# The w_down product of a transformer block by seven block products instead of eight

## The chip, the core and the metric

The kernel runs on one core of a Trainium2 chip. The metric is the time of one launch in device microseconds (us). The engines that matter here are TensorE (PE in the profile, its weight loads PEld), VectorE (DVE), ScalarE (ACT) and the queues that issue DMAs (SP above all). Each engine works through its own list of instructions in order; semaphores hold an instruction until what it needs is there.

## The reference

One layer of a hybrid block, in float32, on 512 tokens of 2048 features. Ahead of the part that is changed stand three mixers (retention, mLSTM, S5), an output projection and a layer norm. The changed part is the feed-forward, and what reads it:

```python
x = layer_norm(ALPHA * x + mix, ln1_w, ln1_b)
ff = jnp.matmul(jnp.square(jax.nn.relu(jnp.matmul(x, w_up))), w_down)
r = ALPHA * x + ff
ple = jax.nn.sigmoid(jnp.matmul(r, w_gate)) * jnp.matmul(p_l, w_ple)
return layer_norm(r + ple, ln2_w, ln2_b)
```

`w_up` is 2048 x 8192, `w_down` 8192 x 2048, `w_gate` 2048 x 2048.

## The kernel before

Activations stand feature-major: a tile is 128 features (partitions) by 512 tokens. Every float32 operand of a large product is split into a high part (a copy by ACT, rounded to the type that TensorE reads, `acp` in `split`, L123) and a low part (a subtraction by DVE, L127), and every product is made of three matmuls, high x high, high x low and low x high (`mm3`, L141 to L143). In them the weight is the stationary operand and 512 tokens of activations move, so a matmul's result is 128 output features by 512 tokens in one PSUM bank.

Weights come as blocks of 128 x 1024 float32 (512 KB), laid out on the host in the order of their use. `wblk` loads one by a DMA on SP's queue (four buffers), and splits it into `wh` and `wl` (three buffers each). One block feeds 24 matmuls. `gemm` runs over blocks.

The feed-forward goes in 16 rounds, `c`. `up(c)` makes four hidden tiles of 128 features in four PSUM banks (tags `mm` and `bu`) from 8 blocks of `w_up`, each of which holds 2 input tiles by 4 hidden tiles; ReLU is ACT's, the square (`tt(r, r, r, MUL)`) and the low part DVE's. `down(c, hs)` takes 8 blocks of `w_down`, two output tiles each, into the banks `wk` and `ya`, and adds each of the 16 banks to its tile `acc[k]` in SBUF by DVE (L114). `acc[k]` held the normed input, so `down(0)` also scales it by ALPHA. `up(c + 1)` is written ahead of `down(c)`, so that TensorE has 192 matmuls (round 0) or 384 (later rounds) of other products between a hidden tile's last matmul and its first use.

After the last round each `acc[k]` is split (`rh`, `rl`) and added to `sd`, the sum over features; the gate product (`gate`, 8 groups) reads all 16 split tiles.

Instructions are put in each engine's list by a list scheduler at build time, from the dependences, the order of writing and the priorities given by `tc.high_priority`; on the chip that list is fixed.

## Time and profile before

| | us |
|---|---|
| median of 3 runs | 2493.32 |
| lowest and highest run | 2492.93, 2493.97 |
| span of the profiled execution, first to last instruction | 2491.1 |
| first matmul on the normed input (feed-forward begins) | 885.2 |
| first matmul of the gate product | 2279.8 |

The profiled execution's time is known by its span; it lies 2.2 us under the median of the runs. The profile's busy time of an engine is the time in which at least one of its instructions is in work. Matmuls overlap, so a busy TensorE need not be at its peak: the distance between the starts of two matmuls says more than their durations. The same holds in a small way for DVE, whose next instruction starts somewhat before the end of the one in work.

### The profile page before, as it was taken

How to read it: one execution, taken by the hardware profiler on the slowest of the kernel's cores; microseconds unless marked ns; L12 is line 12 of the kernel's file. 1: busy time of each engine (PE TensorE's matmuls, PEld its weight loads, DVE VectorE, ACT ScalarE, POOL GpSimd, SP SyncE). 2: the span in 40 equal slices, each digit the busy share in tenths (PEclk: the TensorE clock that was granted, in tenths of full speed). 3: DMA queues.
4: the chain of work that ended last, by engine and by line, in shares of the span. 5: the costliest groups of instructions: out<-in, count | busy, mean ns of one | idle time of the engine just before them, and what ended most of it. 6: DMA issues, size and time to landing. Idle time of an engine off the chain costs nothing.

```text
span 2491.1 us, 29260 instructions
## 1 busy us (share of the span) xinstructions
PE 2454.7 (99%) x11443; PEld 2051.7 (82%) x11443; DVE 1407.6 (57%) x2357; ACT 823.0 (33%) x1187; POOL 89.5 (4%) x182
## 2 busy tenths in 40 slices
PE   9999999999999999999999999999999999999996
PEld 7888888888888878888888888888888888888896
DVE  6788889897654564344334334433433443358477
ACT  4544444444432362122222212222221222123354
POOL 4100000000000000000000000000000000000002
PEclk9999999999999999999999999999999999999998
DMA  6433343333533443333333333332333333233364
GB/s 229 147 107 100 108 121 100 112 100 105 179 119 124 138 127 102 93 101 93 98 98 96 99 94 101 93 101 94 101 94 97 98 94 101 93 102 93 119 188 143
DMA packets 94618, 280.47 MB, mean 113 GB/s; under 512 B 11232, under 2 KB 19856, under 8 KB 94480
## 3 DMA queue, kind: packets, MB, share of 16 engines
q1 hardware_dynamic: 80752, 257.10, 33.1%
q10 hardware_dynamic: 8352, 13.11, 1.6%
q0 software_dynamic: 5376, 8.39, 1.3%
q8 instruction: 90, 1.47, 0.3%
q14 instruction: 48, 0.39, 0.1%
HBM read 264.12 MB, written 14.44 MB: 112 GB/s over the span
## 4 chain that ended last, share of the span: by engine, by line
PE 95%; DVE 2%; DMA 1%; issue 1%; ACT 0%; POOL 0%; ACTq 0%; SPq 0%; DVEq 0%
PE mm L141 14%; PE mm L143 14%; PE mm L142 14%; PE bu L141 7%; PE bu L143 7%; PE bu L142 7%; PE wk L141 7%; PE wk L142 7%; PE wk L143 7%; PE ya L141 2%; PE ya L142 2%; PE ya L143 2%; DMA pldr<-t 1%; PE ya L546 1%; PE wk L620 0%
## 5 line engine op out<-in xcount | busy, mean ns | idle before, releaser
L127 DVE TENSOR_TENSOR wl<-raw,wh 128x1024 fp32r<-128x1024 f32 (+1 forms) x449 | 548.6, 1222 | 641.0 <-ACT wh L123 634.7
L123 ACT ACTIVATE wh<-raw 128x1024 fp32r<-128x1024 f32 (+1 forms) x449 | 474.5, 1057 | 1301.7 <-PE bu L142 573.4
L141 PE MATMUL mm<-xh,wh 128*128 128x512 f32 x800 | 317.3, 397 | 5.5 <-ACT wh L123 5.5
L143 PE MATMUL mm<-xh,wl 128*128 128x512 f32 x800 | 312.9, 391 | 0.0
L142 PE MATMUL mm<-xl,wh 128*128 128x512 f32 x800 | 312.1, 390 | 0.0
L141 PE MATMUL wk<-hh,wh 128*128 128x512 f32 x768 | 298.8, 389 | 0.0
L142 PE MATMUL wk<-hl,wh 128*128 128x512 f32 x768 | 298.8, 389 | 0.0
L143 PE MATMUL wk<-hh,wl 128*128 128x512 f32 x768 | 298.8, 389 | 0.0
L114 DVE TENSOR_TENSOR acc<-acc,wk 128x512 f32<-128x512 f32 (+1 forms) x218 | 142.0, 658 | 151.0 <-PE wk L143 148.4
L141 PE MATMUL mm<-x1h,wh 128*128 128x512 f32 x512 | 200.0, 391 | 1.9 <-ACT t L123 1.9
L142 PE MATMUL mm<-x1l,wh 128*128 128x512 f32 x512 | 199.9, 390 | 0.0
L143 PE MATMUL mm<-x1h,wl 128*128 128x512 f32 x512 | 199.5, 390 | 0.0
L142 PE MATMUL bu<-x1l,wh 128*128 128x512 f32 x512 | 199.2, 389 | 0.0
L143 PE MATMUL bu<-x1h,wl 128*128 128x512 f32 x512 | 199.2, 389 | 0.0
L141 PE MATMUL bu<-x1h,wh 128*128 128x512 f32 x512 | 199.1, 389 | 0.0
L141 PEld LDWEIGHTS mm<-xh,wh 128*128 128x128 f32 x800 | 150.5, 188 | 34.9 <-ACT wh L123 5.5
L143 PEld LDWEIGHTS mm<-xh,wl 128*128 128x128 f32 x800 | 150.4, 188 | 32.0 <-DVE wl L127 0.2
L142 PEld LDWEIGHTS mm<-xl,wh 128*128 128x128 f32 x800 | 150.8, 188 | 29.9
L142 PEld LDWEIGHTS wk<-hl,wh 128*128 128x128 f32 x768 | 144.3, 188 | 29.9
L141 PEld LDWEIGHTS wk<-hh,wh 128*128 128x128 f32 x768 | 144.1, 188 | 30.0
L143 PEld LDWEIGHTS wk<-hh,wl 128*128 128x128 f32 x768 | 144.2, 188 | 29.9
L141 PEld LDWEIGHTS mm<-x1h,wh 128*128 128x128 f32 x512 | 96.5, 189 | 22.4 <-ACT t L123 2.3
(405 smaller groups left out, 3638.5 us busy)
## 6 DMA issues: line engine op xcount, KB each, us to landing
raw<-in_wall_dram SPq DMA_DIRECT2D x447, 512.0 KB, 3.5
xr<-in_xT_dram SPq DMA_DIRECT2D x16, 256.0 KB, 4.3
us<-udr POOLq DMA_DIRECT2D x64, 64.0 KB, 2.3
xr<-in_xT_dram ACTq DMA_DIRECT2D x16, 256.0 KB, 4.0
pldr<-t ACTq DMA_DIRECT2D x16, 256.0 KB, 4.1
out_dram<-acc SPq DMA_DIRECT2D x32, 128.0 KB, 1.8
r<-ydr SPq DMA_DIRECT2D x15, 256.0 KB, 3.8
ydr<-y SPq DMA_DIRECT2D x11, 256.0 KB
```

The source lines that it names most:

```text
L114: (e or V).tensor_tensor(out=out, in0=a, in1=b, op=op)
L123: return A.activation(out=out, in_=in_, func=AF.Copy, scale=scale)
L127: pools["dve"] = V.tensor_tensor(out=lo, in0=x, in1=hi, op=SUB).ins
L141: P.matmul(out=ps, lhsT=wh, rhs=xh, start=start, stop=False)
L142: P.matmul(out=ps, lhsT=wh, rhs=xl, start=False, stop=False)
L143: pools["pe"] = P.matmul(out=ps, lhsT=wl, rhs=xh, start=False, stop=stop).ins
L546: P.matmul(out=yb, lhsT=q["c"][:, j], rhs=z, start=(s % 2 == 0 and n == 0), stop=(s % 2 == 1 and n == 3))
```

## The change

`w_down` is no longer multiplied tile by tile. In each round the hidden tiles are taken as two pairs (`q`), each pair with its tokens in two halves of 256, as a 2 x 2 matrix of blocks A (tokens by hidden features); the matching rows of `w_down` and 1024 of its columns (`p`, two halves) are a 2 x 2 matrix of blocks B. The product of two such matrices is made with seven block products in Winograd's form of Strassen's scheme. It needs four sums of blocks of A (`forms`: S1 to S4, per round and pair) and four differences of blocks of B (`less`, per round and half).

- The seven forms of A, split into `fh` and `fl`, are now stationary, 128 tokens at a time; the weights move, 512 output features at a time. A result is therefore 128 tokens by 512 output features: token-major.
- Each product (`product`) splits one 128 x 1024 block of weights or of a difference of weights, and makes 12 matmuls of it. There are 14 products per round, of 4 + 4 loaded blocks (before: 8 blocks, 24 matmuls each).
- `gather` adds each product's two banks to accumulators `accs` in SBUF. Some banks are added to by a second product without being cleared, and gathered again: 28 gathers per round (before: 16).
- `up(c, g)` makes two hidden tiles at a time from blocks of 4 input tiles by 2 hidden tiles, in two banks (`mm`), and is a generator: one of its four blocks follows every second product. The square is now done by ACT.
- After the last round `result` adds the accumulator `p1` to three others in each half (12 additions), turns each output tile back to feature-major by four transposes on TensorE, adds ALPHA times the normed input and splits the sum. The normed input has been stored to DRAM (`x1dr`) and is loaded again.
- `gate` takes the residual from the split parts: two DVE instructions per tile instead of one.

```diff
-        tt(r, r, r, MUL)
+                A.activation(out=r, in_=r, func=AF.Square)
...
+        nc.sync.dma_start(out=x1dr[k], in_=z)
+    stage.close()
...
+    def up(c, g, hs):
+        b = [bank("mm"), bank("mm")]
+        for i in range(4):
+            wh, wl = wblk(W_UP + (2 * c + g) * 4 + i)
+            for q in range(4):
+                for j in range(2):
+                    k, w = 4 * i + q, slice((2 * q + j) * 128, (2 * q + j + 1) * 128)
+                    mm3(b[j], wh[:, w], wl[:, w], *x1[k], k == 0, k == KT - 1)
+            if i < 3:
+                yield
...
+    def forms(a, b):
+        fh = ffp.tile([128, 7 * T2], F32R, tag="fh", bufs=2, name="fh")
+        fl = ffp.tile([128, 7 * T2], F32R, tag="fl", bufs=2, name="fl")
+        s = ffp.tile([128, 4 * T2], F32, tag="fs", bufs=1, name="fs")
+        p = [s[:, i * T2:(i + 1) * T2] for i in range(4)]
+        tt(p[0], a[:, T2:], b[:, T2:], ADD)
+        tt(p[1], p[0], a[:, :T2], SUB)
+        tt(p[2], a[:, :T2], a[:, T2:], SUB)
+        tt(p[3], b[:, :T2], p[1], SUB)
+        split(a[:, :T2], fh[:, :T2], fl[:, :T2])
+        split(b, fh[:, T2:3 * T2], fl[:, T2:3 * T2])
+        split(s, fh[:, 3 * T2:], fl[:, 3 * T2:])
+        return fh, fl
...
+        def product(form, src, banks, first):
+            with tc.high_priority(2000):
+                wh = whp.tile([128, 1024], F32R, tag="wh", name="wh")
+                wl = wlp.tile([128, 1024], F32R, tag="wl", name="wl")
+                split(src, wh, wl)
+            for t in range(2):
+                o = slice(form * T2 + t * C, form * T2 + (t + 1) * C)
+                for q in range(2):
+                    w = slice(q * S, (q + 1) * S)
+                    (fh, fl), st = fs[q], first and q == 0
+                    for x, y in ((fh, wh), (fh, wl), (fl, wh)):
+                        P.matmul(out=banks[t], lhsT=x[:, o], rhs=y[:, w], start=st, stop=x is fl and q == 1, skip_group_check=not first)
+                        st = False
...
+        ba = [bank("bu"), bank("bu")]
+        product(A11, b11, ba, True)
+        gather("p1", ba)
+        yield
+        less(b12, b12, b11)
+        bc_ = [bank("wk"), bank("wk")]
+        product(S1, b12, bc_, True)
+        gather("c22", bc_)
+        yield
+        less(b12, b22, b12)
+        bb = [bank("ya"), bank("wk")]
+        product(S2, b12, bb, True)
+        gather("c12", bb)
+        yield
+        product(A12, b21, ba, False)
+        gather("c11", ba)
+        yield
+        less(b11, b12, b11)
+        product(S3, b11, bb, False)
+        gather("c22", bb)
+        yield
+        product(S4, b22, bc_, False)
+        gather("c12", bc_)
+        yield
+        less(b21, b21, b12)
+        product(A22, b21, bb, False)
+        gather("c21", bb)
+        yield
...
+    def result(p):
+        for n in ("c12", "c21", "c22"):
+            for t in range(2):
+                tt(accs[p, n, t], accs[p, n, t], accs[p, "p1", t], ADD)
+        for j in range(8):
+            k = 8 * p + j
+            xr = ffp.tile([128, S], F32, tag="r", bufs=4, name="x1r")
+            nc.sync.dma_start(out=xr, in_=x1dr[k])
+            tp = bank("mm")
+            for t in range(NC):
+                src = accs[p, f"c{t // 2 + 1}{j // 4 + 1}", t % 2]
+                P.transpose(tp[:, t * C:(t + 1) * C], src[:, (j % 4) * C:(j % 4 + 1) * C], ident)
+            z = ffp.tile([128, S], F32, tag="r", bufs=4, name="z")
+            stt(z, xr, ALPHA, tp, MUL, ADD)
+            xh, xl = abuf("rh"), abuf("rl")
+            split(z, xh, xl)
...
+            tt(sd, sd, z, ADD)
...
+            d, u = down(c, p, fs), up(c + 1, p, nx) if c + 1 < NF else iter(())
+            for i, _ in enumerate(d):
+                if i % 2 == 0:
+                    next(u, None)
...
-            tt(z, z, nmean[:, sl], ADD)
+            stt(z, rr[k][0][:, sl], 1.0, nmean[:, sl], MUL, ADD)
+            tt(z, z, rr[k][1][:, sl], ADD)
```

In TensorE's list the seam between two rounds reads as follows. Before, the last matmuls of `up` (`x1h`, `x1l` with a `w_up` block) are followed by `down` on hidden tiles (`hh`, `hl`) of the round before:

```order
L142 MATMUL bu_11628<-x1l_8086,wh_11840 128x512
L143 MATMUL bu_11628<-x1h_8085,wl_11841 128x512
L141 MATMUL wk_11897<-hh_11328,wh_11900 128x512
L142 MATMUL wk_11897<-hl_11329,wh_11900 128x512
L143 MATMUL wk_11897<-hh_11328,wl_11901 128x512
```

After, the last matmul of `up` is followed by the first product of the next round, cut in pieces: `fh_11808` and `fl_11809` are the forms of the first pair, `fh_11821` those of the second pair, whose hidden tiles the matmul just ahead has finished; `mm` is the next round's `w_up`.

```order
L143 MATMUL mm_11565<-x1h_8101,wl_11774 128x512
L1029 MATMUL bu_11842<-wh_11844,fh_11808 128x512
L1029 MATMUL bu_11842<-wl_11845,fh_11808 128x512
L1029 MATMUL bu_11842<-wh_11844,fl_11809 128x512
L1029 MATMUL bu_11843<-wh_11844,fh_11808 128x512
...
L141 MATMUL mm_11862<-x1h_7975,wh_11865 128x512
L1029 MATMUL bu_11842<-wh_11844,fh_11821 128x512
L1029 MATMUL bu_11842<-wl_11845,fh_11821 128x512
...
L141 MATMUL mm_11863<-x1h_7984,wh_11865 128x512
L1029 MATMUL bu_11842<-wh_11844,fl_11822 128x512
```

So the first use of a round's last hidden tiles moved from 384 matmuls behind their end to 13 behind it. In all, the seam reads: 6 matmuls of the first product, 7 of `w_up`, 4 of the product, 9 of `w_up`, 2 of the product, 8 of `w_up`, then the second product.

DVE's list at the same seam. Before, it squares and splits four hidden tiles between the splits of weight blocks:

```order
L114 TENSOR_TENSOR r_12413<-r_12413 128x512
L114 TENSOR_TENSOR r_12420<-r_12420 128x512
L127 TENSOR_TENSOR hl_12417<-r_12413,hh_12416 128x512
L114 TENSOR_TENSOR r_12427<-r_12427 128x512
L127 TENSOR_TENSOR wl_12513<-raw_12511,wh_12512 128x1024
```

After (`r_11802`, `r_11805` are the last two hidden tiles; `fs` the sums S1 to S4; `rawd` blocks of `w_down`; `wl_11898` the split for the second product):

```order
L127 TENSOR_TENSOR wl_11866<-raw_11864,wh_11865 128x1024
L127 TENSOR_TENSOR wl_11898<-rawd_11836,wh_11897 128x1024
L114 TENSOR_TENSOR fs_11823<-r_11802 128x256
L114 TENSOR_TENSOR rawd_11836<-rawd_11838,rawd_11836 128x1024
L114 TENSOR_TENSOR fs_11823<-r_11802,r_11805 128x256
L114 TENSOR_TENSOR rawd_11834<-rawd_11836,rawd_11834 128x1024
L114 TENSOR_TENSOR fs_11823<-fs_11823,r_11802 128x256
L127 TENSOR_TENSOR fl_11822<-r_11802,fh_11821 128x256
L114 TENSOR_TENSOR fs_11823<-r_11805,fs_11823 128x256
L127 TENSOR_TENSOR fl_11822<-r_11805,fh_11821 128x512
L114 TENSOR_TENSOR acc_8420<-acc_8420,bu_11842 128x512
```

Two differences of weight blocks and one weight split now stand between the end of the hidden tiles and the low part that TensorE's next pieces need.

DVE's list at the end of the last round. Before, the split and the sum of an output tile (`rl`, `sd`) stand right behind its last addition, among the other additions of the same round:

```order
L114 TENSOR_TENSOR acc_6993<-acc_6993,wk_16589 128x512
L114 TENSOR_TENSOR sd_6429<-sd_6429,acc_6993 128x512
L127 TENSOR_TENSOR rl_16814<-acc_6993,rh_16813 128x512
L114 TENSOR_TENSOR acc_7003<-acc_7003,wk_16590 128x512
L114 TENSOR_TENSOR sd_6429<-sd_6429,acc_7003 128x512
L127 TENSOR_TENSOR wl_16695<-raw_16693,wh_16694 128x1024
```

After, all 16 output tiles stand behind the last gather, one like the next (`mm` holds the transposes, `x1r` the loaded normed input):

```order
L111 SCALAR_TENSOR_TENSOR z_17307<-x1r_17300,mm_17302 128x512
L114 TENSOR_TENSOR sd_6430<-sd_6430,z_17307 128x512
L127 TENSOR_TENSOR rl_17310<-z_17307,rh_17309 128x512
L111 SCALAR_TENSOR_TENSOR z_17321<-x1r_17314,mm_17316 128x512
L114 TENSOR_TENSOR sd_6430<-sd_6430,z_17321 128x512
```

In TensorE's list 60 of the 64 transposes stand behind the last product, and the gate's first matmul behind the last transpose: the gate's two banks are those of the transposes.

## Rows read from the trace of the kernel before

**Rows 1.** The page: busy time of the engines; shares of the chain.
```profile
PE 2454.7 (99%) x11443; PEld 2051.7 (82%) x11443; DVE 1407.6 (57%) x2357; ACT 823.0 (33%) x1187; POOL 89.5 (4%) x182
...
PE 95%; DVE 2%; DMA 1%; issue 1%; ACT 0%; POOL 0%; ACTq 0%; SPq 0%; DVEq 0%
```

**Rows 2.** Groups by line: count, busy us, mean ns, idle before.
```profile
L127 DVE TENSOR_TENSOR wl<-raw,wh 128x1024 fp32r<-128x1024 f32 x447 | 547.2, 1224 | 640.1 <-ACT wh L123 634.0 <-PE ya L546 3.4
L123 ACT ACTIVATE wh<-raw 128x1024 fp32r<-128x1024 f32 x447 | 473.2, 1059 | 1300.7 <-PE bu L142 573.4 <-PE ya L142 258.6 <-PE mm L142 210.9
...
L114 DVE TENSOR_TENSOR acc<-acc,wk 128x512 f32<-128x512 f32 x196 | 133.7, 686 | 149.4 <-PE wk L143 148.4 <-PE wk L870 1.1
...
L123 ACT ACTIVATE hh<-r 128x512 fp32r<-128x512 f32 x64 | 38.7, 632 | 35.4 <-DVE r L114 34.2
```

**Rows 3.** Timeline of TensorE in `up(1)`: start us, us, instruction.
```profile
940.20 0.39 PE L141 MATMUL bu<-x1h,wh 128*128 128x512 f32 x1
...
941.56 0.39 PE L141 MATMUL mm<-x1h,wh 128*128 128x512 f32 x1
```

**Rows 4.** Tiles `x1h` and `rh` on TensorE: ns min/median/max, first and last start.
```profile
L141 PE MATMUL mm<-x1h,wh x512: 389/389/628, 885.2 to 2190.7; 128*128 128x512 f32 x171
...
L141 PE MATMUL mm<-rh,wh x192: 278/283/395, 2279.8 to 2453.6; 128*128 128x256 f32 x128, 128*128 128x512 f32 x64
```

**Rows 5.** Timeline of DVE where it has no wait between instructions.
```profile
975.82 1.23 DVE L127 TENSOR_TENSOR wl<-raw,wh 128x1024 fp32r<-128x1024 f32 x1
976.96 0.69 DVE L127 TENSOR_TENSOR hl<-r,hh 128x512 fp32r<-128x512 f32 x1
977.56 0.68 DVE L111 SCALAR_TENSOR_TENSOR acc<-acc,wk 128x512 f32<-128x512 f32 x1
...
2295.02 3.77 DVE L114 TENSOR_TENSOR acc<-acc,nmean 128x256 f32<-128x256 f32 x11
```

**Rows 6.** Stages: length, then busy us of PE, PEld, DVE, ACT, POOL; clock; DMA.
```profile
1063.00:1500.00 437.00, 437.00 (x1929) 361.97 (x1929) 179.59 (x203) 107.51 (x123) 0.00 (x0) 1.00 0.31 97
```

**Rows 7.** Timeline of DVE while the first norm's tiles become ready.
```profile
901.30 0.68 DVE L127 TENSOR_TENSOR x1l<-acc,x1h 128x512 fp32r<-128x512 f32 x1
901.91 0.74 DVE L111 SCALAR_TENSOR_TENSOR acc<-acc,vv,q 128x512 f32<-128x512 f32 x1
902.57 0.68 DVE L127 TENSOR_TENSOR x1l<-acc,x1h 128x512 fp32r<-128x512 f32 x1
...
912.43 1.46 DVE L127 TENSOR_TENSOR x1l<-acc,x1h 128x512 fp32r<-128x512 f32 x2
```

**Rows 8.** Stages around the start of the feed-forward; the clock is ahead of the DMA share.
```profile
870.00:880.00 10.00, 7.43 (x32) 5.38 (x31) 7.36 (x11) 5.45 (x11) 0.00 (x0) 1.00 0.44 154
880.00:885.00 5.00, 3.31 (x15) 2.28 (x13) 4.71 (x8) 3.51 (x6) 0.00 (x0) 1.00 0.76 239
885.00:890.00 5.00, 4.82 (x14) 3.82 (x15) 2.56 (x4) 2.92 (x6) 0.00 (x0) 0.66 0.79 247
```

**Rows 9.** Timeline of TensorE there; idle us before an instruction in brackets.
```profile
877.44 0.50 PE L141 MATMUL mm<-ph,wh 128*128 128x512 f32 x1 [1.77 <-ACT t L123]
...
885.18 0.50 PE L141 MATMUL mm<-x1h,wh 128*128 128x512 f32 x1 [1.87 <-ACT t L123]
...
886.61 0.63 PE L143 MATMUL mm<-x1h,wl 128*128 128x512 f32 x1
887.03 0.63 PE L141 MATMUL mm<-x1h,wh 128*128 128x512 f32 x1
```

**Rows 10.** Stages at the end of the last round and in the gate, as rows 6.
```profile
2262.00:2280.00 18.00, 18.00 (x81) 14.92 (x80) 16.57 (x23) 7.45 (x11) 0.00 (x0) 1.00 0.36 113
...
2300.00:2320.00 20.00, 20.00 (x90) 16.57 (x89) 8.74 (x12) 5.48 (x8) 0.00 (x0) 1.00 0.43 132
```

**Rows 11.** DMA issues: count, KB each, median us from issue to landing.
```profile
r<-ydr SPq DMA_DIRECT2D x15, 256.0 KB, 3.8
...
xr<-pldr ACTq DMA_DIRECT2D x8, 256.0 KB, 2.9
```

**Rows 12.** Line 602, the transposes of the heads: ns min/median/max.
```profile
L602 PE MATMUL wk<-ident,kT x48: 270/273/328, 83.5 to 653.2; 128*128 128x128 f32 x48
```

More of the change, by code (lines that the diff above doesn't have):

```diff
@@ L200, in hybrid_block_kernel @@
     pldr = dr.tile([KT, 128, S], F32, name="pldr")
+    x1dr = dr.tile([KT, 128, S], F32, name="x1dr")
     def rsqrt(pl, v, n):
@@ L951, in hybrid_block_kernel @@
         x1.append((xh, xl))
-    def up(c):
-        b = [bank("mm"), bank("mm"), bank("bu"), bank("bu")]
-        gemm(W_UP + c * 8, b, x1, 4, 2)
-        hs = []
-        for j in range(4):
-            r = tmp("r", bufs=3)
+        nc.sync.dma_start(out=x1dr[k], in_=z)
+    stage.close()
+    ffp = spool("ff")
+    accs = {}
+    def up(c, g, hs):
[8 more added lines that the diff above has]
+                yield
+        for j in range(2):
+            r = ffp.tile([128, S], F32, tag="r", bufs=4, name="r")
@@ new lines, in up @@
+            hs.append(r)
+        yield
+    T2 = S // 2
+    A11, A12, A22, S1, S2, S3, S4 = range(7)
+    def forms(a, b):
[11 more added lines that the diff above has]
+        return fh, fl
@@ new lines, in down, with gather @@
+    def down(c, p, fs):
+        i = W_DOWN + (2 * c + p) * 4
+        with tc.high_priority(2000):
+            raw = []
+            for j in range(4):
+                t = ffp.tile([128, 1024], F32, tag="raw", bufs=4, name="rawd")
+                nc.sync.dma_start(out=t, in_=wall[i + j])
+                raw.append(t)
+        b11, b12, b22, b21 = raw
+        def product(form, src, banks, first):
+            with tc.high_priority(2000):
+                wh = whp.tile([128, 1024], F32R, tag="wh", name="wh")
[9 more added lines that the diff above has]
+                        st = False
+        def gather(name, banks):
+            for t in range(2):
@@ L980, in down @@
                 with tc.high_priority(400):
-                    if c == 0:
-                        stt(z, z, ALPHA, b[j], MUL, ADD)
-                    else:
-                        tt(z, z, b[j], ADD)
+                    if (p, name, t) not in accs:
+                        z = accs[p, name, t] = ffp.tile([128, S], F32, tag="acc", bufs=20, name="acc")
+                        V.tensor_copy(out=z, in_=banks[t])
+                    else:
+                        z = accs[p, name, t]
+                        tt(z, z, banks[t], ADD)
@@ new lines, in less @@
+        def less(dst, x, y):
+            with tc.high_priority(2000):
+                tt(dst, x, y, SUB)
+        ba = [bank("bu"), bank("bu")]
[11 more added lines that the diff above has]
+        gather("c12", bb)
@@ new lines, in down @@
+        yield
[12 more added lines that the diff above has]
+        gather("c21", bb)
+        yield
+    rr = []
+    def result(p):
+        for n in ("c12", "c21", "c22"):
+            for t in range(2):
+                tt(accs[p, n, t], accs[p, n, t], accs[p, "p1", t], ADD)
[11 more added lines that the diff above has]
+            split(z, xh, xl)
+            rr.append((xh, xl))
+            if k == 0:
+                V.tensor_copy(out=sd, in_=z)
+            else:
+                tt(sd, sd, z, ADD)
@@ L986, in hybrid_block_kernel @@
     NF = FT // 4
-    hs = up(0)
+    hs = []
+    for g in range(2):
+        for _ in up(0, g, hs):
+            pass
     for c in range(NF):
-        nx = up(c + 1) if c + 1 < NF else None
-        down(c, hs)
-        hs = nx
-    rr = []
-    for k in range(KT):
-        xh, xl = abuf("rh"), abuf("rl")
-        split(acc[k], xh, xl)
-        rr.append((xh, xl))
-        if k == 0:
-            V.tensor_copy(out=sd, in_=acc[k])
-        else:
-            tt(sd, sd, acc[k], ADD)
+        fs = [forms(hs[2 * q], hs[2 * q + 1]) for q in range(2)]
+        nx = []
+        for p in range(2):
+            d, u = down(c, p, fs), up(c + 1, p, nx) if c + 1 < NF else iter(())
+            for i, _ in enumerate(d):
+                if i % 2 == 0:
+                    next(u, None)
+        hs = nx
@@ L1003, in hybrid_block_kernel @@
+    result(0)
+    result(1)
+    stage.close()
+    accp = spool("acc2", KT)
+    rp_ = spool("tmp2", 2)
+    acc = [accp.tile([128, S], F32, tag="acc", name="acc") for _ in range(KT)]
+    sq = accp.tile([128, S], F32, tag="sq", bufs=1, name="sq")
     mx = col_mean(sd, "mu")
@@ L1047, in hybrid_block_kernel @@
             nc.sync.dma_start(out=out[k][:, sl], in_=z)
+    stage.close()
 def prep(i):
@@ L1069, in prep @@
     blocks += [_pack(i["s5_glu_w"][0], 2, 4), _pack(w_out, 2, 4), _pack(i["w_ple"][0], 4, 2),
-               _pack(i["w_up"][0], 4, 2)]
-    wd = i["w_down"][0]
-    blocks += [_pack(wd[c * 512:(c + 1) * 512], 2, 4) for c in range(FT // 4)]
+               _pack(i["w_up"][0], 2, 4)]
+    wd = i["w_down"][0].reshape(FT // 4, 2, 2, 128, 2, 2, 512).transpose(0, 4, 2, 5, 3, 1, 6)
+    wd = wd.reshape(FT // 4, 2, 4, 128, 1024)[:, :, [0, 1, 3, 2]]
+    blocks.append(wd.reshape(-1, 128, 1024))
     blocks.append(_pack(i["w_gate"][0], 2, 4))
```

27 lines of the change are left out of this document (8 added, 19 removed).

## The prediction

> **What bounds the kernel now.** The page comes first: TensorE is busy for 99% of the span and holds 95% of the chain that ended last, DVE is busy for 57% and ACT for 33% [rows 1]. A busy TensorE need not be at its peak, so the next view is its timeline: six matmuls after the one at 940.20 the next starts at 941.56, which is 1.36/6 = 0.2267 us from one to the next [rows 3]. The feed-forward has 16 rounds of 384 matmuls, 6144 in all; 6144 x 0.2267 = 1392.8 us. From its first matmul at 885.2 to the gate's first at 2279.8 are 1394.6 us [rows 4]. So there is 2 us of waiting in 1395: the feed-forward is bound by the number of its matmuls, and only fewer matmuls can shorten it. DVE is busy for 179.6 of 437 us there, ACT for 107.5 [rows 6]: 41% and 25%, room for more work. The price of DVE work is its spacing, not its duration: a split of 1024 columns starts at 975.82 and the next instruction at 976.96, 1.14 us; one of 512 takes 0.60; eleven of 256 take 3.77, 0.34 each [rows 5]. The durations are 1.22 and 0.69 [rows 2, 5], some 10% more.
>
> **Matmuls.** Before, w_down took 16 x 8 x 24 = 3072. After, it takes 16 rounds x 2 halves x 7 products x 12 = 2688, of the same shape (128 x 128 stationary, 512 moving, three for one). I give them the same 0.2267 us: **-384 x 0.2267 = -87.1 us**, if TensorE stays the bound. A round then is 360 matmuls, 81.6 us instead of 87.0.
>
> **DVE and ACT per round.** DVE now has 22 weight splits (8 w_up blocks, 14 products) x 1.14 = 25.1, 8 differences `less` of the same size x 1.14 = 9.1, 28 gathers x 0.60 = 16.8, and for two pairs 4 sums x 0.34 and splits of 256, 512 and 1024 columns, 2 x (1.37 + 2.08) = 6.9: together 58 us of 81.6 (64 at full durations). Before it had about 0.41 x 87 = 36. ACT has 22 copies x 1.06 [rows 2], 8 ReLUs and squares at the 0.63 of the copy of 512 [rows 2], and about 4 us of forms: some 33 of 81.6. Both fit on the mean, so away from the seams I cost this at nothing; what hides it is TensorE's 81.6 us. The buffers allow it: three `wh`/`wl`, so a split may start when the third block before it has left TensorE, and has two products (2 x 2.72 us) or a product and a w_up block (8.16 us) to be done.
>
> **The seam between rounds.** This is where cover is thin: 13 matmuls (2.95 us) instead of 384 after the last hidden tile. Let 0 be the end of the last w_up matmul. ACT: first ReLU done at 0.1, the copy for the second product (1.06) to 1.3, second ReLU 1.7, squares 2.8, first form of the second pair 3.1. TensorE has run 13 matmuls by 2.95 and waits 0.2; then 4 + 9 more to 6.1. DVE, in its listed order: the split for the second product from 1.3 to 2.45, then three sums (0.34 each), two differences (1.14 each) and the first form's low part (0.34), up to 6.15; TensorE waits 0.1. The low part of S1 is ready at 9.5; the second product asks for it at 9.6. I take **0.4 us per seam, 15 x 0.4 = +6**. Bounds: 0, and 2.2, because from the end of the last product of a round (-5.2) to the split for the next w_up block (10.6) DVE has 14.8 us of work in 15.8 us; at full durations it is late by 1.8 more. So 0 to +33.
>
> **The first w_up product.** It asks for two hidden tiles at a time, so it passes the 16 normed input tiles in 96 matmuls, 21.8 us, from 885.2 to 907.0; before, four at a time, in 43.5 us. DVE delivers one input tile every 1.27 us (901.30 to 902.57) plus a weight split every four, 1.55 against TensorE's 1.36, and the last one came at 913.9 [rows 7]. With the last six matmuls the product ends between 908 (+1) and 915.3 (+8); a clock that falls on the way could make it +13. DVE's idle moments there go away, so I take **+6**.
>
> **The last round and the result.** The last round has no w_up beside it: 168 matmuls, 38.1 us, against DVE's 13 splits (14.8), 8 differences (9.1), 28 gathers (16.8), the second pair's forms (3.4), three splits for the gate (3.4) and six of the twelve additions of `result` (3.6) = 51.1 us, and DVE's list has them all ahead of the first output tile. Then 16 tiles in a chain: DVE's sum 0.69, ACT's copy 0.63, DVE's low part 0.69 (`sd` fits into ACT's time), 2.07 with the hand-overs, 33; the other six additions 3.6; less 1.3, as the gate needs only the last tile's sum and then its split. Together 51.1 + 33.1 + 3.6 - 1.3 = 86.5, and 1.5 for the loads of `x1r`: with four buffers tile k + 2's load starts when tile k is summed, and 256 KB took 2.9 or 3.8 us [rows 11]; at 3.8 a tile takes (3.8 + 0.8)/2 = 2.3. So 88 us stand against 38.1: **+50**. The 64 transposes (0.27 each, 17 us [rows 12]) lie beside DVE's chain. Before, the same splits and sums ran under the last round, in which TensorE was never idle (18.0 of 18.0 us, DVE 16.6 [rows 10]). Bounds +45 (DVE's spacing alone) and +57 (loads of 3.8 us, full durations).
>
> **Clock.** At 870 to 880 TensorE was idle for 2.6 of 10 us and kept the granted clock of 1.00; after 1.7 more idle us and the 1.87 ahead of 885.18 it was at 0.66 in the next 5 us [rows 8, 9], and matmuls followed each other at 0.42 us instead of 0.227. Seven to nine of them cost 1.4 to 1.8 us. In the result stage TensorE works under half the time, so the gate may start at the lower of its two levels, 1.2 GHz: **+1.5** (0 to 2).
>
> The gate's extra instruction per tile, 16 x 0.6 us, falls where DVE is busy for 8.7 of 20 us [rows 10]; the stores and loads of the normed input are 32 transfers of 256 KB where the DMA engines are busy for 0.31 [rows 6]: nothing for either, unless the last gate groups are reached with a backlog, a few us.
>
> **Sum.** -87.1 + 6 + 6 + 50 + 1.5 = -23.6; the 2 us of waiting in the old feed-forward go too, as the seams count all waiting now: -25. On the profiled span of 2491.1 this is 2466; the runs lie 2.2 above it: **2468**.
>
> **A rule weighed.** The Trainium skill, "TensorE: Matmul & The Clock Gate", section "HAM oscillation — how this bites in real kernels", says that TensorE's clock is gated down when it idles and has to be earned again, and that a loop that makes it wait once per turn pays this once per turn. This speaks against the change, which puts a wait at every seam. The trace agrees that the clock falls after idling [rows 8], but the 1.77 us of idling ahead of 877.44 did not bring it down [rows 9]. By the rule, once per seam, the time would be that of the second rival below; by the rows, that of the sum.
>
> **Rivals.**
> *DVE late at the seam (slower).* Its list puts two differences and a weight split, 3.4 us, between the hidden tiles and the low part that TensorE's 27th matmul behind the seam needs. If DVE comes to the seam with a backlog of that size, since two gathers and 2.1 us of the first pair's splits, which wait for the last product, stand just ahead, every seam costs 3.4 more: 15 x 3.4 = 51, 2519. It turns the gain into a loss from 0.4 + 25/15 = 2.1 us per seam. For it: 14.8 of 15.8 us. Against: DVE idles 1.3 us at the seam for ACT, and has 24 spare us per round to catch up. Chance 0.15; a backlog of half the size, about 2493, 0.10.
> *The clock falls at each seam.* If TensorE's wait there brings its clock to the lower level, a seam costs 1.6 us as ahead of 890 [rows 8, 9]: 15 x 1.6 = 24, 2492, no change. Against: an idle 1.77 us did not do it, and these waits are tenths; chance 0.06.
> *The result overlaps with the last round.* If TensorE's list did not hold the transposes behind all products, most of the 50 us would go: some 2425. The list speaks against it, and DVE has no room in that round; chance 0.07.
> *As forecast*, TensorE-bound rounds and an exposed end: 2450 to 2488, chance 0.62.
>
> **Range and chances.** Faster by over 0.2% (about what a measurement of this kernel can tell from no change, 5 us) is the forecast and the overlapped result, 0.69; within 0.2% are the half backlog and the clock, 0.16; slower 0.15. The ends of all bounds together give -40 to +20; a range from 2448 to 2505 leaves out the overlapped result and most of the late DVE, under 2 in 10.
>
> **What would show it.** Right: a round of 82 us, TensorE's waits at the seam behind ACT's or DVE's `fh`, `fl` and under 1 us; DVE near 70% in the rounds; 35 to 50 us in which TensorE is mostly idle ahead of the gate's first matmul, with DVE and ACT alternating; the gate's first matmul near 2252. Wrong: a spacing of the new matmuls other than 0.227; rounds of 84 us or more, with TensorE waiting for `wl` or for gathers in mid-round; a first w_up product over 35 us long; a last stage longer than 215 us from the gate's first matmul.

## The result and the profile after

The changed kernel takes **2466.2 us** (median of 4 runs, 2465.8 to 2466.5) against 2493.2 (2492.9 to 2494.0) for the kernel of before: a ratio of 0.9889, 95% interval 0.9875 to 0.9903. The forecast was 2468. Three executions further below that took far longer than the others of their kernel (one of sd_pe, 3033 us, and two of pad32, 8590 and 13,793 us) are left out of the medians and ratios. The profiled execution spans 2464.2 us, 26.9 less than the 2491.1 of before.

The page of the changed kernel; the lines answer to [rows 1]:

```profile
PE 2401.5 (97%) x11123; PEld 1989.7 (81%) x11123; DVE 1810.0 (73%) x2921; ACT 978.8 (40%) x1379; POOL 89.3 (4%) x182
...
PE 92%; DVE 5%; issue 1%; DMA 1%; ACT 1%; POOL 0%; ACTq 0%; DVEq 0%
```

TensorE has lost 53 us of busy time and 2 points of the span; DVE has gained 402 us and gone from 2% to 5% of the chain. So TensorE still bounds the kernel nearly everywhere, and there is one new place in which DVE does. Tiles `x1h`, `fh` and `rh` on TensorE (first and last start at the end of the numbers) cut the feed-forward into stages, as [rows 4] did:

```profile
L141 PE MATMUL mm<-x1h,wh x1024: 387/389/632, 884.5 to 2167.9; 128*128 128x512 f32 x171
...
L1029 PE MATMUL bu<-wh,fh x256: 388/392/505, 935.7 to 2203.9; 128*128 128x512 f32 x128
...
L1029 PE MATMUL wk<-wl,fh x448: 388/394/502, 944.3 to 2212.4; 128*128 128x512 f32 x150
...
L141 PE MATMUL mm<-rh,wh x192: 278/283/764, 2250.5 to 2426.7; 128*128 128x256 f32 x128, 128*128 128x512 f32 x64
```

The first hidden tiles take from 884.5 to the first product at 935.7, 51.2 us. The last w_up matmul, third of its train, starts at 2168.3; from 935.7 to there are 15 rounds of (2168.3 - 935.7)/15 = 82.17 us (with starts read to 0.1 us, good to 0.01). From 2168.3 to the gate's first matmul at 2250.5 are 82.2 us, and 213.7 more to the end. Stages of the changed kernel, columns as in [rows 6] (length, busy us of PE, PEld, DVE, ACT, POOL, clock, DMA share, GB/s): one round, and two parts of the stage behind the last round's products.

```profile
1022.00:1104.00 82.00, 82.00 (x361) 67.28 (x360) 58.76 (x73) 30.92 (x36) 0.00 (x0) 1.00 0.33 103
...
2200.00:2225.00 25.00, 14.93 (x61) 10.70 (x60) 24.40 (x37) 6.56 (x7) 0.00 (x0) 0.86 0.32 95
2225.00:2256.00 31.00, 18.87 (x62) 12.92 (x63) 28.30 (x44) 8.84 (x14) 0.00 (x0) 0.50 0.40 112
```

In a round TensorE is busy for all 82 us at the full granted clock, and DVE for 58.8 (72%) where it had 41% [rows 6]. At the end the picture turns over: DVE is busy for 24.4 of 25 and 28.3 of 31 us, TensorE for about 60%, at a granted clock that has fallen to 0.50. DVE and ACT in that result stage, in order of time:

```profile
2245.72 0.68 DVE L111 SCALAR_TENSOR_TENSOR z<-x1r,mm 128x512 f32<-128x512 f32 x1
...
2246.44 0.63 ACT L123 ACTIVATE rh<-z 128x512 fp32r<-128x512 f32 x1 [1.35 <-DVE z L111]
2246.44 0.69 DVE L114 TENSOR_TENSOR sd<-sd,z 128x512 f32<-128x512 f32 x1
2247.10 0.69 DVE L127 TENSOR_TENSOR rl<-z,rh 128x512 fp32r<-128x512 f32 x1
2247.71 0.68 DVE L111 SCALAR_TENSOR_TENSOR z<-x1r,mm 128x512 f32<-128x512 f32 x1
```

One tile is a chain: its sum (0.72 with the hand-over), ACT's copy beside `sd` (0.66), the low part (0.61), 1.99 us from sum to sum.

### The profile page after: what moved, and what is told of

Its sections match the earlier page's. It is cut to its first block, busy times and chain, and to the rows that moved or that the text cites. A ratio compares the mean times of both kernels' runs of the same rounds, so it can differ in the third digit from the quotient of the medians.

```text
span 2464.2 us, 29505 instructions
## 1 busy us (share of the span) xinstructions
PE 2401.5 (97%) x11123; PEld 1989.7 (81%) x11123; DVE 1810.0 (73%) x2921; ACT 978.8 (40%) x1379; POOL 89.3 (4%) x182
## 4 chain that ended last, share of the span: by engine, by line
PE 92%; DVE 5%; issue 1%; DMA 1%; ACT 1%; POOL 0%; ACTq 0%; DVEq 0%
PE mm L141 19%; PE mm L142 19%; PE mm L143 19%; PE wk L1029 12%; PE bu L1029 7%; PE ya L1029 5%; PE bu L141 3%; PE bu L142 3%; PE bu L143 3%; DVE wl L127 1%; DVE acc L114 1%; PE ya L547 1%; DVE acc L111 1%; PE wk L621 0%; PE wk L603 0%
## 5 line engine op out<-in xcount | busy, mean ns | idle before, releaser
L141 PE MATMUL mm<-x1h,wh 128*128 128x512 f32 x1024 | 398.3, 390 | 3.7 <-ACT x1h L123 2.2
L142 PE MATMUL mm<-x1l,wh 128*128 128x512 f32 x1024 | 399.5, 390 | 0.6 <-DVE x1l L127 0.6
L143 PE MATMUL mm<-x1h,wl 128*128 128x512 f32 x1024 | 399.2, 390 | 0.0
L123 ACT ACTIVATE wh<-rawd 128x1024 fp32r<-128x1024 f32 x224 | 237.0, 1060 | 320.9 <-PE wk L1029 225.5
L127 DVE TENSOR_TENSOR wl<-rawd,wh 128x1024 fp32r<-128x1024 f32 x224 | 272.9, 1220 | 120.8 <-ACT wh L123 120.8
L142 PEld LDWEIGHTS mm<-x1l,wh 128*128 128x128 f32 x1024 | 192.5, 188 | 42.5 <-DVE x1l L127 1.9
L143 PEld LDWEIGHTS mm<-x1h,wl 128*128 128x128 f32 x1024 | 192.5, 188 | 40.4
L1029 PE MATMUL wk<-wl,fh 128*128 128x512 f32 x448 | 176.4, 394 | 0.7 <-DVE wl L127 0.7
L1029 PE MATMUL wk<-wh,fh 128*128 128x512 f32 x448 | 175.3, 392 | 0.7 <-ACT wh L123 0.7
L1029 PE MATMUL wk<-wh,fl 128*128 128x512 f32 x448 | 174.1, 389 | 0.0
```

The lines of the kernel that those rows point to most:

```text
L123: return A.activation(out=out, in_=in_, func=AF.Copy, scale=scale)
L127: pools["dve"] = V.tensor_tensor(out=lo, in0=x, in1=hi, op=SUB).ins
L141: P.matmul(out=ps, lhsT=wh, rhs=xh, start=start, stop=False)
L142: P.matmul(out=ps, lhsT=wh, rhs=xl, start=False, stop=False)
L143: pools["pe"] = P.matmul(out=ps, lhsT=wl, rhs=xh, start=False, stop=stop).ins
L1029: P.matmul(out=banks[t], lhsT=x[:, o], rhs=y[:, w], start=st, stop=x is fl and q == 1, skip_group_check=not first)
```

## The experiments

All kernels are edits of the changed kernel. The table has each kernel's ratio to the kernel of before with its 95% interval, and from its profiled execution the same stages as above: to the first product, a round, from the last w_up matmul to the gate's first, and from there to the end.

| kernel | median us | ratio to before | first tiles | round | end of rounds to gate | gate to end |
|---|---|---|---|---|---|---|
| changed kernel | 2466.2 | 0.9889 [0.9875, 0.9903] | 51.2 | 82.17 | 82.2 | 213.7 |
| no_less | 2460.5 | 0.9871 [0.9855, 0.9888] | 51.4 | 82.15 | 76.5 | 213.5 |
| load_seam | 2487.5 | 0.9976 [0.9965, 0.9987] | 51.6 | 83.27 | 86.7 | 214.5 |
| load_mid | 2468.0 | 0.9897 [0.9882, 0.9912] | 50.9 | 82.21 | 82.1 | 213.2 |
| classical8 | 2542.2 | 1.0195 [1.0179, 1.0210] | 51.3 | 87.6 | 76.5 | 213.4 |
| early_result | 2467.9 | 0.9892 [0.9875, 0.9909] | 51.5 | 82.21 | 82.3 | 216.2 |
| last_classical | 2460.8 | 0.9869 [0.9855, 0.9884] | 51.5 | 82.22 | 75.9 | 215.8 |
| sd_pe | 2483.9 | 0.9966 [0.9955, 0.9976] | 51.6 | 82.89 | 88.9 | 213.5 |
| sd_pe_pipe | 2485.9 | 0.9967 [0.9954, 0.9980] | 51.4 | 82.89 | 89.2 | 215.7 |
| pad32 | 2479.3 (2 runs) | 0.9949 [0.9929, 0.9969] | 51.5 | 82.85 | 82.5 | 216.6 |
| best_nopool | 2450.1 | 0.9832 [0.9816, 0.9848] | 44.8 | 82.23 | 72.5 | 213.0 |
| best_pool | 2457.0 | 0.9860 [0.9845, 0.9874] | 44.9 | 82.22 | 76.5 | 214.9 |
| best_shift | 2449.6 | 0.9829 [0.9810, 0.9848] | 43.6 | 82.23 | 72.5 | 214.7 |

In classical8 one product of 2.7 us still follows the last w_up matmul of a round; that is taken into its round. The last column is nearly the same code in every row (sd_pe and sd_pe_pipe take the mean from TensorE's banks, best_pool from POOL's sum), so its 213.0 to 216.6 show the scatter of one execution. In five of them (early_result, last_classical, pad32, best_pool, best_shift) the granted clock is at 0.50 for a short stretch late in the gate. A difference of 2 us in a total is not read as an effect below; the other columns of kernels that do not touch a stage agree much better.

### Does DVE's work per round count? (no_less)

```diff
         def less(dst, x, y):
-            with tc.high_priority(2000):
-                tt(dst, x, y, SUB)
+            pass
```

> The changed kernel without its 128 differences `less` (the products then take the loaded blocks as they are, so the result is another one). DVE does 8 x 1.14 = 9.1 us less per round. Theory (TensorE bounds the rounds, DVE only the last one): a round stays at 82.0 to 82.2 us; the last round, where DVE sets the end, loses its 9.1, and the seams up to 0.2 x 15 = 3: 2466.2 - 12 = about 2454. Rival (DVE paces the rounds): up to 16 x 9.1 = 146 us less, near 2320, and anything below 2440 speaks for it.

Measured: 2460.5, rounds of 82.15. Taking 9.1 us of DVE work out of each round leaves the round as it was: TensorE paces it, and "DVE paces the rounds" is out. The effect, 5.7 us, lies behind the last w_up matmul. That is less than the 9.1 I expected, because TensorE's own matmuls become the limit there. Its last product matmul starts 39.8 us behind that w_up matmul instead of 44.3, close to the 38.5 of 168 matmuls at 0.2293, and DVE, idle for 2.1 of the 50.8 us up to its first output sum in the changed kernel, is idle for 4.4 of 45.0.

### Is the seam really thin? (load_seam, load_mid)

```diff
                 if i % 2 == 0:
                     next(u, None)
+            if p == 1:                       # load_mid: p == 0
+                for _ in range(3):
+                    for h in nx[2 * p:2 * p + 2]:
+                        tt(h, h, h, MAX)
```

> The changed kernel with 6 extra DVE instructions of 0.60 us per round (the maximum of a hidden tile with itself, 3 times each), on the second pair's hidden tiles, ahead of their sums and splits: 3.6 us just behind the last w_up matmul, in 15 rounds. Theory (DVE has no room at the seam): nearly all of it shows, 3.4 to 3.6 us per seam, +51 to +54, near 2518, the time that the prediction gave to a DVE that is late by 3.4 us. Rival (DVE has 23 spare us per round, so work is hidden wherever it stands): +0 to +5.

> The same 6 extra DVE instructions of 0.60 us per round, 3.6 us, on the first pair's hidden tiles, which are ready half a round before the seam. Theory (it is the place and not the sum of DVE's work that counts): +0 to +3. Rival (DVE's total per round counts): the same +51 to +54 as with the load at the seam.

Load_mid is the changed kernel again (rounds 82.21): 3.6 us more DVE work in mid-round cost nothing, so DVE's total does not matter. The same work at the seam costs, but 1.1 us per round, +21 us in all (16.5 in the rounds, 4.5 in the last), not 51 to 54. The place counts, as the theory said; its price per round was three times too high. Why shows on TensorE. The changed kernel's seam, from the last w_up matmul of a round, with DVE's split for the second product:

```profile
1017.68 0.39 PE L143 MATMUL mm<-x1h,wl 128*128 128x512 f32 x1
1017.91 0.39 PE L1029 MATMUL bu<-wh,fh 128*128 128x512 f32 x1
...
1019.01 1.23 DVE L127 TENSOR_TENSOR wl<-rawd,wh 128x1024 fp32r<-128x1024 f32 x1 [2.36 <-ACT wh L123]
1019.28 0.39 PE L141 MATMUL mm<-x1h,wh 128*128 128x512 f32 x1
...
1020.87 0.49 PE L1029 MATMUL bu<-wh,fh 128*128 128x512 f32 x1
1021.20 0.39 PE L1029 MATMUL bu<-wl,fh 128*128 128x512 f32 x1
...
1026.33 0.39 PE L1029 MATMUL wk<-wh,fh 128*128 128x512 f32 x1
```

and that of load_seam:

```profile
1016.21 0.39 PE L143 MATMUL mm<-x1h,wl 128*128 128x512 f32 x1
1016.44 0.39 PE L1029 MATMUL bu<-wh,fh 128*128 128x512 f32 x1
...
1017.81 0.39 PE L141 MATMUL mm<-x1h,wh 128*128 128x512 f32 x1
...
1023.25 0.39 PE L1029 MATMUL wk<-wh,fh 128*128 128x512 f32 x1
...
1024.65 0.50 PE L1029 MATMUL bu<-wh,fh 128*128 128x512 f32 x1
...
1028.60 0.50 PE L1029 MATMUL wk<-wh,fh 128*128 128x512 f32 x1 [0.69 <-ACT fh L123]
```

In the changed kernel the first matmul on the second pair of hidden tiles (1020.87) stands 13 matmuls behind the last w_up matmul, and the one behind it comes 0.10 us late: 0.33 us after it instead of 0.23. Such a step stands once at every seam, and no other step between two product matmuls is over 0.29 in the 15 rounds. The whole of the 36 matmuls up to 1026.33 takes 8.42 us instead of 36 x 0.2267 = 8.16; the other 0.16 us is a slightly wider spacing. In load_seam the first matmul on the second pair stands 36 matmuls behind (1024.65), because all 24 of the next w_up block, and the first pair's part of the second product, were moved ahead of it. The order was made with the extra work in it, and the cover grew with it. At the seam into the last round, where no w_up block is left to move ahead, the load cost 4.5 us, its full 3.6 and more. What a delay costs that the order does not know of (a late DMA, a slower DVE) is not shown by this pair.

### What does the seventh product buy? (classical8)

In short: eight products, with the forms A11, A21, A12, A22 and the blocks as loaded; `less`, the sums of forms and `p1` fall away.

```diff
-        fs = [forms(hs[2 * q], hs[2 * q + 1]) for q in range(2)]
+        fs = [forms4(hs[2 * q], hs[2 * q + 1]) for q in range(2)]
...
-            d, u = down(c, p, fs), ...
+            d, u = down8(c, p, fs), ...    # B11: c11, c21; B21: c11, c21; B12: c12, c22; B22: c12, c22
```

> The changed kernel with eight block products per pair in place of seven, all else kept: hidden tiles stationary, weights moving, the sum in four tiles per half, transposed back, interleaved with w_up. No sums and differences of blocks, no p1 and its additions, 4 weight splits and 8 gathers of one tile per half round. Theory (matmuls set the rounds; the new arrangement costs about 60 us by itself): 24 more matmuls per round, 15 x 24 x 0.228 = +82; the last round 43.8 us on TensorE and the result 16 x 2 us behind it, 76 in place of 82; seams up to -4: 2466 + 82 - 6 - 4 = 2538, so some 45 us over the kernel of before. Rival (the arrangement is nearly free, and the seventh product saves little): 2495 to 2505.

Measured 2542.2 (theory 2538). The arrangement that makes room for the seven products (stationary hidden tiles, a result that is transposed back, the first tiles two at a time) costs 2542.2 - 2493.2 = 49 us by itself; leaving out one product in eight takes back 76. The 27 us of gain are the difference of these two. The 49 lie where the table has them: 7.7 in the first tiles (51.2 against 192 x 0.2267 = 43.5), 15 x 0.55 = 8 in the rounds (87.6 against 384 x 0.2267 = 87.05), and 33 at the end (76.5 against 43.5). So most of the price of the arrangement is the result, which stands behind the products with nothing beside it.

### What sets the end? (early_result, last_classical, sd_pe, sd_pe_pipe)

```diff
+            if c == NF - 1 and p == 0:
+                result(0)
...
-    result(0)
```

> The changed kernel with the first half's result (8 of the 16 output tiles: transposes, sums, splits) written between the two halves of the last round, no longer behind both. From the last w_up matmul to the gate's first were 82 us, in which DVE is busy for 87 of 92. Theory (DVE's work sets the end, so its order does not matter): 0 to -4. Rival (the transposes' place behind all products is what costs): 8 tiles x 1.99 = -16.

82.3 us against 82.2, the time unchanged, as the theory said, but the run proves less than it was meant to. The list hardly moved: of the 64 transposes two stand 7 us earlier, and DVE makes its first output sum 50.8 us behind the last w_up matmul as before (2169.5 to 2220.31; 2168.3 to 2219.10). The gathers and the weight splits carry a priority and the result does not, so while DVE has a backlog of those, the result comes last wherever it is written. That the result's place in the program is not the cause is shown; what a real overlap would bring is not.

```diff
-        fs = [forms(hs[2 * q], hs[2 * q + 1]) for q in range(2)]
+        last = c == NF - 1
+        fs = [(forms4 if last else forms)(hs[2 * q], hs[2 * q + 1]) for q in range(2)]
...
-            d, u = down(c, p, fs), ...
+            d, u = (down8 if last else down)(c, p, fs), ...
```

> The changed kernel with eight block products instead of seven in the last round alone, where no w_up work hides DVE's sums: DVE does some 26 us less there (6 splits, 8 differences, 12 gathers, the sums of the hidden tiles), TensorE 24 more matmuls (5.4). Theory: DVE's work set the end of that round, so the end comes earlier in spite of more matmuls; the eight-product kernel took 79.2 us from its last w_up matmul to the gate, without p1 and its additions, against 82.2, so -3 to 0, if the additions find room in the round. Rival (the number of matmuls counts there too): +5.

75.9 us against 82.2: **24 more matmuls in the last round make the end 6.3 us shorter** (the medians, 2460.8 and 2466.2, lie 5.4 apart). That is DVE's bound shown from the other side. My -3 was too cautious: I had taken 79.2 us from classical8 without seeing that 2.7 of it were a product of the round before. Groups of DVE in that round, with idle time at the end:

```profile
L114 DVE TENSOR_TENSOR acc<-acc 128x512 f32<-128x512 f32 x11 | 7.4, 688 | 0.1
L127 DVE TENSOR_TENSOR wl<-rawd,wh 128x1024 fp32r<-128x1024 f32 x6 | 7.3, 1225 | 13.4 <-ACT wh L123 13.4
```

DVE now idles for 13 us ahead of its splits, and 11 of the 12 additions of `result` fit under the round, behind TensorE.

```diff
-            if k == 0:
-                V.tensor_copy(out=sd, in_=z)
-            else:
-                tt(sd, sd, z, ADD)
+            for t in range(NC):
+                P.matmul(out=mus[t][:, :1], lhsT=z[:, t * C:(t + 1) * C], rhs=onec, start=k == 0, stop=k == KT - 1)
```

> The changed kernel with the running sum `sd` of the 16 output tiles taken off DVE: TensorE adds each tile's column sums with 4 matmuls against a column of ones, kept in 4 banks. DVE does 16 x 0.60 = 9.6 us less in the result. Theory (a tile's chain, sum on DVE, copy on ACT, low part on DVE, 1.99 us, sets the pace, and `sd` lay inside ACT's time): 0 to -2. Rival (DVE's total work sets the pace): -9.6.

This went wrong in two ways that neither theory had: 2483.9, with rounds of 82.89 (next section) and 88.9 us at the end. DVE and TensorE of this kernel in the result stage:

```profile
2238.67 0.68 DVE L111 SCALAR_TENSOR_TENSOR z<-x1r,mm 128x512 f32<-128x512 f32 x1
...
2239.14 1.09 PE L1091 MATMUL mm<-ident,acc 128*128 128x128 f32 x4
...
2240.03 0.85 PE L1098 MATMUL bu<-onec,z 128*128 128x1 f32 x4
2240.05 0.69 DVE L127 TENSOR_TENSOR rl<-z,rh 128x512 fp32r<-128x512 f32 x1 [0.70 <-ACT rh L123]
2240.66 0.68 DVE L111 SCALAR_TENSOR_TENSOR z<-x1r,mm 128x512 f32<-128x512 f32 x1
...
2241.60 1.09 PE L1091 MATMUL mm<-ident,acc 128*128 128x128 f32 x4
```

DVE's rows answer the question: without `sd` a tile still takes 1.99 us (2238.67 to 2240.66), and where `sd` stood DVE waits 0.70 us for ACT. So the chain set the pace, as the theory said, and `sd` was free. But the four column sums take TensorE 1.57 us at a granted clock of 0.50 (2240.03 to 2241.60), where I had put 0.4 (I had read the 8 records of `col_mean`, 0.81 us at 1.00, as 8 matmuls; they are 4), so TensorE needs 2.46 per tile and becomes the bound: from the sixth tile on DVE's sums are 2.45 apart. In sd_pe_pipe, with the chain opened, the same 2.46 hold, and it says nothing on the chain:

```diff
-            split(z, xh, xl)
+            acp(xh, z)
+            low.append((xl, z, xh))
+            if k > 0:
+                tt(*low[k - 1], SUB)
```

> As the kernel with `sd` on TensorE, and each tile's low part is written behind the next tile's sum, so that DVE does not wait for ACT's copy within a tile; the tiles' sums stand in the freed buffers of the weights. A tile then takes DVE 0.60 + 0.60 us, and TensorE 1.11 for the transposes and some 0.4 for the column sums. Theory (the chain set the pace): 16 x (1.99 - 1.5) = 8 less, and up to 2 more, -6 to -10. Rival (loads of x1r or TensorE at its lower clock set the pace): 0 to -3.

89.2 us at the end: neither theory, for the reason just given. The chain was opened again in best_nopool, with `sd` left on DVE.

### 32 bytes (pad32, best_shift)

Rounds of 82.89 in sd_pe could not come from an edit behind the rounds. Its order in the rounds is the same; what differs is that one small tile more, in a pool ahead, moved the tiles of the feed-forward's pool by 32 bytes.

```diff
     sd = bp.tile([128, S], F32, name="sd")
+    bp.tile([128, 8], F32, name="pad")
```

> The changed kernel with an unused tile of 32 bytes per partition in a pool ahead, so that the hidden tiles' forms, the loaded w_down blocks and the sums lie 32 bytes further in SBUF, as they did in the two kernels with the column sums on TensorE; nothing else is changed. Those kernels' rounds took 82.89 us in place of 82.17 although the rounds' lists were the same, and the 12 matmuls of a product 2.80 us in place of 2.74. Theory (the place of the operands in SBUF sets the spacing of the product's matmuls): rounds of 82.9, +0.72 x 15 and as much in the last round, +11, near 2477. Rival (something else in those kernels): 2466.

Rounds of 82.85, and a ratio of 0.9949 to before instead of 0.9889: an unused tile costs 0.6%, half of the change's gain. TensorE in pad32 and in the changed kernel, the first and a later matmul of a product:

```profile
1050.26 0.39 PE L1030 MATMUL wk<-wh,fh 128*128 128x512 f32 x1
...
1052.83 0.40 PE L1030 MATMUL wk<-wh,fl 128*128 128x512 f32 x1
```

```profile
1048.21 0.39 PE L1029 MATMUL wk<-wh,fh 128*128 128x512 f32 x1
...
1050.27 0.39 PE L1029 MATMUL wk<-wh,fh 128*128 128x512 f32 x1
```

Eleven steps in 2.57 us are 0.2336 each; nine in 2.06 are 0.2289 (over the 15 rounds, 0.2334 and 0.2293). The w_up matmuls between them, none of whose operands moved, step at 0.227 in both kernels. Before, the trains went at 0.2267 [rows 3]. Is the new place bad by itself, or only against that of the weights?

```diff
+    cp.tile([128, 8], F32, name="pad")
     hpi = cp.tile([128, 1], F32, name="hpi")
```

> The fastest kernel so far (eight products in the last round, first hidden tiles four at a time, low parts behind the next sum: 2450.1 us) with an unused tile of 32 bytes per partition at the start of its first pool, so that all tiles move by 32 bytes, the weights and the input tiles as well as the forms. It tells what the 32 bytes did in the kernel where the forms alone moved (82.85 us per round for 82.17). Theory (the place of the stationary operand against the moving one counts, and that is as it was): rounds of 82.2, 2450. Rival 1 (the place of the stationary operand by itself counts, and the new place is the worse one): the matmuls of w_up, of the input projections and of the gate slow down too, by about 0.005 each, some 50 us in 10,600: near 2500. Rival 2 (operands that all begin at a multiple of 64 bytes are read faster): every matmul gains, by up to a few per cent, 2400 or less.

2449.6 against 2450.1, rounds of 82.23 in both: with all tiles moved by the same 32 bytes the loss is gone. So it is not the place of a tile by itself that counts but its place relative to tiles that stayed where they were in pad32, and of the operands of the slower matmuls these are the stationary one (`fh`, `fl`), which moved, and the moving one (`wh`, `wl`), which did not. The tiles that DVE and ACT use beside them (`rawd`, `fs`, `acc`) moved with `fh`; that they have no part in it is not shown. Which distances are good, and whether one gives the 0.2267, was not tried.

### A faster version (best_nopool, best_pool)

Three edits: last_classical, the opened chain of sd_pe_pipe, and the first round's hidden tiles four at a time, in four banks, over twice as long a pass through the normed input:

```diff
-    for g in range(2):
-        for _ in up(0, g, hs):
-            pass
+    up4(hs)        # banks mm, mm, bu, bu; last weight block tile by tile
```

> Three changes on the changed kernel: eight products in the last round (measured alone: 82.2 to 75.9 us from the last w_up matmul to the gate); the first hidden tiles of round 0 computed four at a time, since TensorE waits there for the 16 normed tiles (51.2 us for 192 matmuls that need 43.5); each result tile's low part written behind the next tile's sum. Theory: 2460.75, less 5 to 7 for the first tiles, less 16 x (1.99 - 1.8) = 3 for the result, as DVE's three instructions of 0.60 then follow each other without waiting: 2451. Rival: the first products wait for all four hidden tiles at once, and lose 3 to 5 of that; 2455.

> The same with the running sum `sd` on POOL, so that DVE has two instructions of 0.60 per result tile. Theory: a tile takes 1.3 in place of 1.8, 16 x 0.5 = 8 less than the kernel with `sd` on DVE: 2443. Rival (POOL's addition is slower than a tile's 1.3 us, and TensorE waits for the mean early in the gate): the end of POOL's chain takes the place of DVE's, no gain or a loss, 2451 to 2460.

**2450.1 us**, 0.9832 [0.9816, 0.9848] of the kernel of before: 43 us below it and 16 below the changed kernel. The first tiles take 44.8 instead of 51.2, the 192 x 0.2267 = 43.5 that their matmuls need and 1.2 for six steps at the lower clock (0.43 us each), which confirms that TensorE waited there, for the normed tiles and for a bank (the shares stand with the first w_up product, below). A result tile takes 1.80 us, three DVE instructions without a gap (the rows below): the chain is gone, DVE's sum remains. From the end of the rounds to the gate are 72.5 us.

```profile
2217.29 0.68 DVE L114 TENSOR_TENSOR rl<-zz,rh 128x512 fp32r<-128x512 f32 x1
2217.89 0.68 DVE L114 TENSOR_TENSOR sd<-sd,zz 128x512 f32<-128x512 f32 x1
2218.49 0.68 DVE L114 TENSOR_TENSOR rl<-zz,rh 128x512 fp32r<-128x512 f32 x1
```

With `sd` on POOL the end takes 4.0 us more, not 8 less (76.5 against 72.5; the medians lie 6.9 apart). DVE and POOL of best_pool there (x2: two instructions):

```profile
2217.47 2.94 POOL L114 TENSOR_TENSOR sd<-sd,zz 128x512 f32<-128x512 f32 x2 [1.29 <-DVE zz L111]
2217.84 3.10 DVE L114 TENSOR_TENSOR rl<-zz,rh 128x512 fp32r<-128x512 f32 x2
2220.87 1.27 DVE L111 SCALAR_TENSOR_TENSOR zz<-x1r,mm 128x512 f32<-128x512 f32 x2
...
2222.07 3.13 DVE L114 TENSOR_TENSOR rl<-zz,rh 128x512 fp32r<-128x512 f32 x2
```

Beside POOL's additions (1.47 each) DVE's low parts take 1.55 us instead of 0.60, while its sums, which read one operand from PSUM, keep their 0.6. Two tiles take 4.23, so 2.1 each. The rival's time came (2451 to 2460), but not by its mechanism: POOL does not lag, it slows DVE. The Trainium skill, "SBUF — State Buffer", section "🔬 SBUF: two separate sides", says that DVE and GpSimd share one pair of ports as an exclusive lock, which a DVE instruction with two SBUF inputs needs too; the trace agrees, with 1.55 us for the instruction that has two and 0.6 for the one that has one.

## Why the prediction was right, point by point

- **Matmuls, -87.1.** The count came as put, the spacing not quite. Over the 15 rounds a product's matmuls follow each other in 0.2293 us in place of 0.2267 (classical8: 0.2292), some 0.42 us per round and 6.3 in all. The step that failed is "I give them the same 0.2267 us": the roles of stationary and moving operand were exchanged and new tiles placed. Pad32 shows that the place is a price of its own; how much of the 6.3 it makes, and how much the exchange, is not shown.
- **DVE and ACT in the rounds, nothing.** 58.8 us of DVE where the sum gave 58, 30.9 of ACT where it gave 33; no_less and load_mid show that they are hidden.
- **The seam, +6.** Rounds of 82.17 are 0.57 over 360 x 0.2267 = 81.6: 0.42 is the spacing above, 0.05 a wider spacing of w_up matmuls, and only 0.10 is waiting at the seam, where I had put 0.4. The timeline there goes as worked out, including DVE's order of split, sum, difference. Together 15 x 0.57 = +8.6, near the +6 by luck: the waiting was put 4.5 too high over 15 seams, and the spacing, put at nothing, cost 6.3.
- **The first w_up product, +6.** 51.2 - 43.5 = +7.7. The cause was right in the main: some 4.9 of it are waits for the normed tiles, the longest in the first row below. Two parts are of another kind: 1.6 for a bank, which ReLU of the first pair has to free before the second pair begins (the second row, and what restarting costs), and 1.2 for six steps at the lower clock, of which the kernel before has some too [rows 9]. Best_nopool, with four banks and half the pace through the tiles, keeps only the last.

```profile
PE mm L141 <- ACT x1h L123: 2.2, 1, 2.2
PE mm L141 <- ACT r L983: 1.4, 1, 1.4
```

- **The last round and the result, +50.** 82.2 - 38.1 = +44.1. DVE's first output sum came 50.8 us behind the last w_up matmul (2219.10), where 51.1 were put. What was too long is the chain behind it, 31.4 us in place of 36.9: the gate's first matmul waits for the bank of the tile before the last, so it starts 1.2 us ahead of the last tile's sum, where I had it 0.8 behind that sum's start (1.9); a tile took 1.99 and not 2.07 (15 x 0.08 = 1.2); the 1.5 for the loads were not paid, since 256 KB of `x1r` landed in 2.6 us (the line is below); and some of the additions hid under ACT's copy (0.8).

```profile
x1r<-x1dr SPq DMA_DIRECT2D x16, 256.0 KB, 2.6
...
2249.69 0.68 DVE L111 SCALAR_TENSOR_TENSOR z<-x1r,mm 128x512 f32<-128x512 f32 x1
...
2250.52 0.76 PE L141 MATMUL mm<-rh,wh 128*128 128x512 f32 x1 [0.96 <-DVE z L111]
...
2251.68 0.68 DVE L111 SCALAR_TENSOR_TENSOR z<-x1r,mm 128x512 f32<-128x512 f32 x1
...
2255.76 0.40 PE L141 MATMUL mm<-rh,wh 128*128 128x512 f32 x1
```

- **Clock, +1.5.** The gate starts at a granted clock of 0.50, 1.2 GHz: its first twelve steps, to 2255.76, take 5.24 us where twelve at 0.227 take 2.72. That is 2.5, over the bound of 2, since twelve matmuls stand in it where seven to nine were put; it makes up the stage's 213.7 us against 211.3, +2.4. TensorE was not mostly idle ahead of it, as the forecast's sign had it, but busy for 60%, and the clock was at 0.50 all the same. One reading of the rows before was wrong: the 1.7 us of idle time up to 885 are the beginning of the 1.87 ahead of 885.18, not time besides it.
- **The sum.** -87.1 + 8.6 + 7.7 + 44.1 + 2.4 = -24.3; the 2 us of waiting in the old feed-forward go too, and the feed-forward starts 0.7 earlier: -27.0, against 26.9 on the span. The total came within 2 us partly because terms missed in opposite directions: three were 5 us too small together (spacing and seams, first product, clock and gate), one 6 too large. That is luck on top of a mechanism that was right.
- **The rivals.** A DVE that is late at the seam did not come: it had no backlog there, and idled 2.36 us for ACT ahead of its split (1019.01). The place is sensitive, as load_seam shows, but 3.6 us more of work cost 1.1 per round, with an order made for it, so the break-even of 2.1 us per seam was farther away than it looked. The clock did not fall at the seams: 1.00 from 890 to 2215 us; so the Trainium skill's rule on loops that wait once per turn ("TensorE: Matmul & The Clock Gate", "HAM oscillation — how this bites in real kernels") was no price here, where a wait is 0.10 us. The overlapped result did not come, and early_result shows that writing it earlier does not bring it about.

## What to carry to other kernels

Price a trade of matmuls for vector work stage by stage: under a long train of matmuls DVE may go from 41% to 72% for nothing, and the same work costs its full time in the one round that has no other work beside it, where the version with more matmuls can be the faster one. At an end that runs tile by tile, count one tile's chain through the engines before taking work off the busiest of them: `sd` lay in a wait and was free. And before a small gain is believed or given up, look at the spacing of the matmuls themselves: moving a tile by 32 bytes was worth half of this change.
